# Column-group products in a different order: conditioning steps, state space outputs and the last gate

## Chip, core, metric

One Trainium2 chip, one core. The metric is the device time of one execution of the whole block in microseconds (us); the time before is the median of three runs, 1891.27 us.

## What is computed

A transformer-like block over 256 tokens and 2048 features, all in fp32. Cut to what the change touches:

```python
cond = silu(c) @ w_ada + b_ada                       # 2048 -> 6 x 2048
sh1, sc1, g1, sh2, sc2, g2 = split(cond, 6)
h = rmsnorm(x, norm1_g) * (1 + sc1) + sh1
u, q, kv, gates = split(h @ w_in, ...)
# state space mixer: (sr, si) is a complex scan along the 256 tokens
y = einsum('ghp,blgp->blgh', c_re, sr) - einsum('ghp,blgp->blgh', c_im, si) + d_skip * u
z = gelu(y); y_ssm = z * sigmoid(z @ w_glu + b_glu)
y_att = nsa_attention(q, kv, gates)                  # compressed, selected and window branches
x = x + g1 * (concat(rmsnorm(y_ssm), rmsnorm(y_att)) @ w_out)
h2 = rmsnorm(x, norm2_g) * (1 + sc2) + sh2
x = x + g2 * peer(h2)                                # 16384 experts, top 16 of each of 8 heads
out = rmsnorm(x, final_g)
```

## The kernel before

The large products are made exact to fp32 by splitting each operand into two fp32r parts, hi and lo, and adding three products (hi hi, hi lo, lo hi). A weight unit of 128x1024 is loaded by the SP queue into a ring of four `raw` buffers, ScalarE casts hi (L99), VectorE subtracts for lo (L102), TensorE multiplies (L521, L582, L775, L1013).

Three kinds of products have few output rows and are plain fp32, which the hardware runs as two passes each:

- **Conditioning, `cond_job` (L441 to L458).** `silu(c)` is one vector, so each product has one useful output row. Column k of it stands in `scz` as a 128x32 stationary with zeros behind it, and the product of group g goes to PSUM partitions 32g to 32g+31 (`cps`). So four products, which belong to four slices of the contraction, use four different 32-column groups of the array; L475 or L468 adds the four rows later. A job (j, q) gives 512 of the 12288 outputs; it has four steps of four products, and each step reads two loaded units of 512 KB: `tiles[0:2]` come from unit p2, `tiles[2:4]` from unit p2+1 (`load_steps`, L418). 20 jobs make 80 steps. The units of the first jobs lie in several borrowed buffers (`adap`, `er`, `vN`, `hi`, `lo`, `adax`), those of the last twelve jobs in the three buffers `adap` alone. The first eight jobs are needed early, for `h`; the twelve others are fed in between other work by `pump`.
- **State space outputs, `s5_py` (L699).** One step handles four of 64 state groups. VectorE makes four rotated products p, q, a2, c2 in this order (L683 to L686, tiles `s1`, `s3`, `s4`, `s5`), GpSimd and VectorE share what comes before. Each of the four then gives a pair of 128*32 products into two column groups of `py` (L710): 16 steps of four pairs.
- **The last gate, `g2_job` (L1313).** The vector is the stationary itself (128x1), and four products go to PSUM partitions 0, 32, 64 and 96 (`psg`, L1318). Products 0 and 1 read the first unit `rs[0]`, products 2 and 3 the second unit `rs[1]`, both in the `raw` ring. There are 16 such steps, put between the tiles of the expert scores (`u_tile`, products `pa` of L521, with the gate groups `g_group`, `pgs` L1290).

What sets the order of work is the build itself: the program is recorded in the order in which Python runs it, and a scheduler with a simulated timeline then orders each engine's instructions by when their operands are ready on that timeline. TensorE, VectorE, ScalarE, GpSimd and the SP load queue each execute their own list strictly in that order. So a line that is written in another order moves rows on all engines.

Of the kernel before, what the change touches and what calls it, by code (L numbers as in the profile page):

```python
# [60 lines left out]
def build(tc, A):  # L61
    nc = tc.nc

    def bc(ap, shape):
        return ap.to_broadcast(list(shape))
# [20 lines left out]
    def unit(src, pool=None, tag="raw", bufs=4):  # L86
        if pool:
            r = pool.tile([128, 1024], F32, name=tag, tag=tag, bufs=bufs)
        else:
            r = buf("raw")  # L90
        i = nc.sync.dma_start(r, src)
        if tag.startswith("ada"):
            last["ada"] = i.ins
        return r
# [323 lines left out]
    def load_steps(n):  # L418
        while len(loaded) < min(n, len(loads)):
            s = len(loaded)  # L420
            j, q, p2 = loads[s]
            r = min(s // 8, len(rings) - 1)
            tiles = []
            for p in (p2, p2 + 1):
                b = rings[r][turns[r] % len(rings[r])]
                turns[r] += 1
                src = A["w_ada"][j, q, p]
                if isinstance(b, tuple):
                    x = unit(src, *b)
                    tiles += [x[:, :512], x[:, 512:]]  # L430
                else:
                    xs = spare(b)
                    for i, x in enumerate(xs):
                        w = 1024 // len(xs)
                        last["ada"] = nc.sync.dma_start(x, src[:, i * w:(i + 1) * w]).ins
                    tiles += xs if len(xs) == 2 else [xs[0][:, :512], xs[0][:, 512:]]
            loaded.append(tiles)
# [3 lines left out]
    def cond_job(j, q, late=0, ahead=0):  # L441
        ps = psM.tile([128, 512], F32, name="cps", tag="cps", bufs=1)
        for kt in range(0, KT, 4):
            load_steps(min(ran[0] + 1 + ahead, 32) if ahead else ran[0] + 1)
            tiles = loaded[ran[0]]
            assert loads[ran[0]] == (j, q, kt // 2)
            ran[0] += 1
            for g in range(4):
                nc.tensor.matmul(ps[32 * g:32 * g + 32, :], scz[:, kt + g], tiles[g],  # L449
                                 start=kt == 0, stop=kt == KT - 4)  # L450
            if kt == KT - 4:
                rows = base1.tile([128, 512], F32, name="rows", tag="rows", bufs=1)
                nc.scalar.copy(rows, ps)
            yield
        if late:
            finish.append([late, j, q, rows])
        else:
            cond_end(j, q, rows)  # L458
# [3 lines left out]
    def cond_end(j, q, rows):  # L462
        if j == 2:
            b = base1.tile([1, 1024], F32, name="row", tag="adap", bufs=3)[:, :512]
            cs = slice(q * 512, (q + 1) * 512)
            nc.gpsimd.dma_start(b, A["b_row"][0:1, cs])
            ps = psM.tile([1, 512], F32, name="psr", tag="mm", bufs=1)
            nc.tensor.matmul(ps, sel4, rows, start=True, stop=True)  # L468
            nc.vector.tensor_tensor(out=b, in0=b, in1=ps, op=OP.add)
            nc.gpsimd.dma_start(g1d[:, cs], b)  # L470
        else:
            i = {0: 0, 1: 1, 3: 2, 4: 3}[j]
            ps = psM.tile([128, 4], F32, name="pscol", tag="mm", bufs=1)
            for b in range(4):
                nc.tensor.matmul(ps[:, b:b + 1], rows[:, b * 128:(b + 1) * 128], sel4, start=b == 0, stop=b == 3)  # L475
            ks = slice(4 * q, 4 * q + 4)
            o = cond[:, i, ks]
            nc.vector.tensor_tensor(out=o, in0=ps, in1=bada[:, j, ks], op=OP.add)
            if j in (1, 4):
                nc.vector.scalar_tensor_tensor(o, o, 1.0, ng[:, j // 4, ks], op0=OP.add, op1=OP.mult)  # L480
# [11 lines left out]
    for j in (1, 0):  # L492
        for _ in cond_job(j, 0, ahead=4):
            pass
    h_quarter(0)

    def jobs(todo):
        for j, q in todo:
            yield from cond_job(j, q, late=2)
# [92 lines left out]
    def parts():  # L592
        for q in range(1, 4):
            for j in (1, 0):
                yield from cond_job(j, q, ahead=3)
            h_quarter(q)
# [18 lines left out]
    quad = {}  # L615

    def tl(tag):
        return s5t.tile(SHP, F32, name=tag, tag=tag, bufs=1)

    def rot(j0):  # L620
        return [bc(E[:, j0:j0 + 2].unsqueeze(2), SHP) for E in (Er, Ei)]
# [35 lines left out]
    def s5_out(n):  # L657

        jq, half = divmod(n, 2)
        j0 = 2 * n  # L660
        a, c = quad.pop(n)
        w = s5t.tile([128, 2, 2, 2], F32, name="zi0", tag="zi0", bufs=2)

        def scans(h):
            for ri, src in enumerate((a, c)):
                for i in range(2):
                    init = 0.0 if h == 0 else w[:, 1, ri, i:i + 1]
                    v.tensor_tensor_scan(out=src[:, i, h], data0=bc(mag[:, j0 + i:j0 + i + 1], [128, 128]),
                                         data1=src[:, i, h], initial=init, op0=OP.mult, op1=OP.add)
        scans(0)  # L670
        zr1, zi1 = a[:, :, 0, 127], c[:, :, 0, 127]
        c1, s1 = E128[:, 0, j0:j0 + 2], E128[:, 1, j0:j0 + 2]
        t = s5t.tile([128, 2, 2], F32, name="zt", tag="zt", bufs=2)
        v.tensor_tensor(out=w[:, 0, 0], in0=zr1, in1=c1, op=OP.mult)
        v.tensor_tensor(out=w[:, 0, 1], in0=zi1, in1=s1, op=OP.mult)
        v.tensor_tensor(out=t[:, 0], in0=zr1, in1=s1, op=OP.mult)
        v.tensor_tensor(out=t[:, 1], in0=zi1, in1=c1, op=OP.mult)
        v.tensor_tensor(out=w[:, 1, 0], in0=w[:, 0, 0], in1=w[:, 0, 1], op=OP.subtract)
        v.tensor_tensor(out=w[:, 1, 1], in0=t[:, 0], in1=t[:, 1], op=OP.add)
        scans(1)  # L680
        er, ei = rot(j0)
        p, q, a2, c2 = tl("s1"), tl("s3"), tl("s4"), tl("s5")
        v.tensor_tensor(out=p, in0=a, in1=er, op=OP.mult)  # L683
        v.tensor_tensor(out=q, in0=c, in1=ei, op=OP.mult)
        v.tensor_tensor(out=a2, in0=a, in1=ei, op=OP.mult)
        v.tensor_tensor(out=c2, in0=c, in1=er, op=OP.mult)  # L686
        quad["pq", n] = (0, p), (2, q), (1, a2), (1, c2)

    zs = {"todo": [], "go": False}

# [105 lines left out]
    def s5_step(k):  # L796

        if k < 16 and k % 2 == 0:
            quad["CP", k // 2] = s5_c(k // 2)
        late = k < 16 and k not in POOL_PAIRS and k and k - 1 not in POOL_PAIRS  # L800
        if k < 16 and k not in POOL_PAIRS and not late:
            s5_in(k)
        if k + 1 in POOL_PAIRS:
            s5_in(k + 1)
        if k:
            s5_out(k - 1)
            done.append(k - 1)
        while done:
            s5_py(done.pop())
        if late:  # L810
            s5_in(k)
# [280 lines left out]
    for k in range(0, KT, 2):  # L1092
# [7 lines left out]
        for i in range(2):  # L1100
            p = ps[:, i].rearrange("p a t -> p (a t)")
# [211 lines left out]
    def g2_job():  # L1313
        for kt in range(KT):
            rs = [unit(A["w_g2"][kt * 128:(kt + 1) * 128, h * 1024:(h + 1) * 1024])
                  for h in range(2)]
            for g in range(4):
                nc.tensor.matmul(g2ps[32 * g:32 * g + 1, :], scol[:, kt:kt + 1],  # L1318
                                 rs[g // 2][:, g % 2 * 512:(g % 2 + 1) * 512], start=kt == 0, stop=kt == KT - 1)
            yield  # L1320

    def g2_end(pool):
        rows = pool.tile([128, 512], F32, name="g2r", tag="g2r")
        for g in range(4):
# [3 lines left out]
            nc.gpsimd.dma_start(g2d[:, cs], rows[r])  # L1328

    g2 = g2_job()  # L1330
    while state["t"] < T:
        for _ in range(2):
# [408 lines left out]
```

## Time and profile before

| what | value |
|---|---|
| three runs | 1888.39, 1891.27, 1891.78 us, median 1891.27 |
| the profiled execution, its own time | 1887.95 us |
| its span, first to last instruction | 1886.1 us |
| TensorE (PE) busy | 1781.8 us, 94% |
| VectorE (DVE) busy | 1381.6 us, 73% |
| ScalarE (ACT), GpSimd (POOL) busy | 804.6 and 824.4 us |
| mean granted TensorE clock | 0.978 of 2.4 GHz |
| moved by DMA | 436.8 MB, 232 GB/s on average |

A row of the timeline gives start and duration; matmuls overlap, so what one costs TensorE is the distance from its start to the start of the next one. In time the kernel goes: 0 to 50 us first conditioning jobs and the transposes of x; 50 to 160 first half of the input projection with six more jobs; 160 to 400 the rest of it with the state space steps and the compression; 400 to 600 attention, output projection and the last conditioning jobs; 600 to 880 the expert queries and the first expert score tiles; 880 to 1312 score tiles with gate groups and the g2 steps; then the last score tiles, and from 1420 us on the gathered expert values.

### The profile page before, as it was taken

The numbers are of one execution on the slowest core, as the hardware profiler recorded it, in microseconds if no ns is written. First come the engines' busy times: TensorE is split into PE (matmuls) and PEld (weight loads), VectorE is DVE, ScalarE is ACT, GpSimd is POOL, SyncE is SP. The second block draws the span as 40 slices with busy tenths as digits, with TensorE's granted clock in tenths as the row PEclk, the third lists the DMA queues.
The fourth block names the chain that finished last, engine by engine and source line by source line (L and its number), as shares of the span: only waits on it lengthen the run. The fifth ranks groups of instructions, "written<-read, shape, count | busy, mean of one in ns | idle before, by whom it ended". The sixth has DMA issues, their size and how long they took to land. (4 is left out here: it accounts for less than half of the span.)

```text
span 1886.1 us, 32604 instructions
## 1 busy us (share of the span) xinstructions
PE 1781.8 (94%) x12048; PEld 1488.0 (79%) x12048; DVE 1381.6 (73%) x2765; ACT 804.6 (43%) x1329; POOL 824.4 (44%) x926
## 2 busy tenths in 40 slices
PE   5999999999999899999999999999998999999895
PEld 2756655568666899999999898898998898777674
DVE  3636998756745698888999898998783457776666
ACT  3422211148634544444444444444432336555554
POOL 5923432201110210112787666665027665887532
PEclk9998999999999999999999999999998999999998
DMA  9987556785686455555565556556567779999972
GB/s 358 407 286 265 192 185 226 260 314 199 238 268 208 166 180 179 171 178 167 184 194 193 190 183 196 184 178 201 182 186 218 227 233 356 323 326 323 373 258 109
DMA packets 117839, 436.77 MB, mean 232 GB/s; under 512 B 17237, under 2 KB 19989, under 8 KB 107686
## 3 DMA queue, kind: packets, MB, share of 16 engines
q1 hardware_dynamic: 91440, 322.41, 51.3%
q0 software_dynamic: 22080, 108.62, 16.2%
q10 hardware_dynamic: 4150, 3.56, 0.6%
q8 instruction: 97, 1.59, 0.3%
q14 instruction: 72, 0.59, 0.1%
HBM read 411.38 MB, written 23.15 MB: 230 GB/s over the span
## 5 line engine op out<-in xcount | busy, mean ns | idle before, releaser
L102 DVE TENSOR_TENSOR lo<-raw,hi 128x1024 fp32r<-128x1024 f32 x382 | 512.9, 1345 | 229.6 <-ACT hi L99 188.3
L99 ACT CAST hi<-raw 128x1024 fp32r<-128x1024 f32 x385 | 402.1, 1047 | 590.7 <-PE pa L521 302.2
L521 PE MATMUL pa<-hhi,lo 128*128 128x256 f32 x2048 | 590.3, 288 | 10.1 <-DVE lo L102 6.7
L521 PE MATMUL pa<-hhi,hi 128*128 128x256 f32 x2048 | 583.6, 285 | 9.7 <-ACT hi L99 6.8
L521 PE MATMUL pa<-hlo,hi 128*128 128x256 f32 x2048 | 583.1, 285 | 0.0
L521 PEld LDWEIGHTS pa<-hhi,lo 128*128 128x128 f32 x2048 | 395.0, 193 | 38.3 <-DVE lo L102 11.1
L521 PEld LDWEIGHTS pa<-hhi,hi 128*128 128x128 f32 x2048 | 395.3, 193 | 10.8 <-ACT hi L99 8.0
L521 PEld LDWEIGHTS pa<-hlo,hi 128*128 128x128 f32 x2048 | 395.3, 193 | 0.5 <-issue 0.5
L1287 POOL TENSOR_TENSOR mv<-o,gp 128x256 fp32r<-128x256 f32 x256 | 186.4, 748 | 124.9 <-DVE o L1284 65.8
L1505 DVE TENSOR_TENSOR lv<-rv,hv 128x1024 fp32r<-128x1024 f32 x144 | 173.1, 1229 | 55.7 <-ACT hv L1504 52.3
L1504 ACT CAST hv<-rv 128x1024 fp32r<-128x1024 f32 x144 | 146.3, 1049 | 63.6 <-DMA rv<-in_peer_v,wt 40.7
L1284 DVE TENSOR_TENSOR o<-pT,iota 128x256 fp32r<-128x256 f32 (+1 forms) x256 | 124.8, 502 | 30.8 <-PE pgs L1290 17.9
L449 PE MATMUL cps<-adap,scz 128*32 128x512 f32 x476 | 113.8, 622 | 16.4 <-DMA adap<-in_w_ada 16.4
L1205 POOL TENSOR_TENSOR eq<-eq,iff 128x512 f32<-128x512 f32 x16 | 30.0, 1896 | 212.1 <-DVE eq L1204 212.1
L1305 POOL TENSOR_TENSOR SA<-SA,gs 128x50 f32<-128x50 f32 (+42 forms) x128 | 113.8, 904 | 12.9 <-ACT SA L1162 12.5
L1414 POOL DMA_INDIRECT wc<-SA,slot x88 | 97.1, 1103 | 46.1 <-issue 25.2
L1459 POOL DMA_INDIRECT rv<-in_peer_v,wt x74 | 97.3, 1316 | 45.2 <-DVE lv L1505 17.5
L521 PE MATMUL lin<-hhi,hi 128*128 128x256 f32 x352 | 104.8, 298 | 2.2 <-ACT sg L998 1.3
L521 PE MATMUL lin<-hlo,hi 128*128 128x256 f32 x352 | 102.9, 292 | 1.5 <-POOL hlo L1111 1.0
L521 PE MATMUL lin<-hhi,lo 128*128 128x256 f32 x352 | 102.6, 292 | 0.0
L1295 ACT COPY gs<-pgs 128x256 f32<-128x256 f32 x128 | 47.6, 373 | 121.7 <-POOL SA L1305 107.5
L521 PEld LDWEIGHTS lin<-hhi,hi 128*128 128x128 f32 x352 | 68.1, 194 | 26.3 <-issue 16.9
(450 smaller groups left out, 3291.9 us busy)
## 6 DMA issues: line engine op xcount, KB each, us to landing
raw<-in_peer_u SPq DMA_DIRECT2D x256, 512.0 KB
adap<-in_w_ada SPq DMA_DIRECT2D x119, 512.0 KB
raw<-in_w_in SPq DMA_DIRECT2D x32, 512.0 KB
raw<-in_w_out SPq DMA_DIRECT2D x32, 512.0 KB
raw<-in_peer_wq SPq DMA_DIRECT2D x32, 512.0 KB
raw<-in_w_g SPq DMA_DIRECT2D x32, 512.0 KB
raw<-in_w_inq SPq DMA_DIRECT2D x16, 512.0 KB
raw<-in_cmp_w SPq DMA_DIRECT2D x16, 512.0 KB
```

Source lines behind the costliest of these rows:

```text
L99: i = nc.scalar.copy(hi[:, :n], raw[:, :n])
L102: (lo_engine or nc.vector).tensor_tensor(out=lo[:, :n], in0=raw[:, :n], in1=hi[:, :n].bitcast(F32), op=OP.subtract)
L449: nc.tensor.matmul(ps[32 * g:32 * g + 32, :], scz[:, kt + g], tiles[g], start=kt == 0, stop=kt == KT - 4)
L521: nc.tensor.matmul(ps, w, a[:, kk], start=first and u == 0 and k == 0 and i == 0, stop=last and u == n - 1 and k == 7 and i == 2)
L1284: nc.vector.tensor_tensor(out=o, in0=bc(pT[:, j, t:t + 2].unsqueeze(2), shp), in1=io, op=OP.is_equal)
L1287: nc.gpsimd.tensor_tensor(out=mv[:, :, j], in0=o2, in1=g, op=OP.mult)
L1295: nc.scalar.copy(tmp, pv[:, 1])
L1305: nc.gpsimd.tensor_tensor(out=o, in0=o, in1=tmp[:, a0:m], op=OP.mult)
L1414: d = nc.gpsimd.indirect_dma_start(out=wcs[i], out_offset=bass.IndirectOffsetOnAxis(ap=ap, axis=0), in_=SB[:, m - NSA] if i else SA[:, m], ...
L1459: d = nc.gpsimd.indirect_dma_start(out=raw, out_offset=None, in_=A["peer_v"], in_offset=bass.IndirectOffsetOnAxis(ap=wt[:, 128:129].bitcas ...
L1504: nc.scalar.copy(hi, raw)
L1505: state["last"] = nc.vector.tensor_tensor(out=lo, in0=raw, in1=hi.bitcast(F32), op=OP.subtract).ins
```

## The change

Three loops are written in another order. In the conditioning step and in the g2 step the two products of the second unit come first, then those of the first: groups 2, 3, 0, 1. In the state space step the pair of c2, which VectorE makes last, comes first: c2, p, q, a2. Which products there are and what each reads and writes is the same; only `start` and `stop` follow the same step numbers as before, and the sum of the four state space pairs is taken in another order.

```diff
@@ cond_job @@
-            for g in range(4):
+
+            for g in (2, 3, 0, 1):
                 nc.tensor.matmul(ps[32 * g:32 * g + 32, :], scz[:, kt + g], tiles[g],
                                  start=kt == 0, stop=kt == KT - 4)
@@ s5_out @@
-        quad["pq", n] = (0, p), (2, q), (1, a2), (1, c2)
+        quad["pq", n] = (1, c2), (0, p), (2, q), (1, a2)
@@ g2_job @@
-            for g in range(4):
+            for g in (2, 3, 0, 1):
                 nc.tensor.matmul(g2ps[32 * g:32 * g + 1, :], scol[:, kt:kt + 1],
                                  rs[g // 2][:, g % 2 * 512:(g % 2 + 1) * 512], start=kt == 0, stop=kt == KT - 1)
```

The lines after the first edit move down by one (L449 becomes L450, L710 L711, L1318 L1319).

TensorE in the g2 stage, the first of 16 steps (the others moved in the same way). `psg` are the g2 products (raw_9167 is the first unit, raw_9169 the second), `pa` the score products. Before, the first pair:

```order
L521 MATMUL pa_8983<-hhi_90,hi_8979 128x256
L521 MATMUL pa_8983<-hlo_91,hi_8979 128x256
L1318 MATMUL psg_8840<-raw_9167,scol_77 1x512 x2
L521 MATMUL pa_8983<-hhi_90,lo_8980 128x256
L521 MATMUL pa_8983<-hhi_90,hi_8979 128x256
```

and, 26 rows after it, the second:

```order
L1290 MATMUL pgs_8848<-mv_8843,o1_8841 128x256 x2
L521 MATMUL pa_8983<-hhi_90,lo_8980 128x256
L521 MATMUL pa_9081<-hhi_90,hi_9071 128x256
L521 MATMUL pa_9081<-hlo_91,hi_9071 128x256
L1318 MATMUL psg_8840<-raw_9169,scol_77 1x512 x2
L521 MATMUL pa_9081<-hhi_90,lo_9072 128x256
```

Now:

```order
L522 MATMUL pa_9081<-hhi_90,hi_9071 128x256
L522 MATMUL pa_9081<-hlo_91,hi_9071 128x256
L1291 MATMUL pgs_8848<-mv_8843,o1_8841 128x256 x2
L1319 MATMUL psg_8840<-raw_9169,scol_77 1x512 x2
L1319 MATMUL psg_8840<-raw_9167,scol_77 1x512 x2
L522 MATMUL pa_9081<-hhi_90,lo_9072 128x256
L522 MATMUL pa_9081<-hhi_90,hi_9071 128x256
```

All four products stand next to each other, near the place where the second pair stood.

TensorE in the attention stage, steps of conditioning job cps_4084, before (`lin` is the output projection, `ppt`, `plg`, `psq` are attention and norm products):

```order
L978 MATMUL psq_4511<-ones_92,sqt_4080 128x1
L449 MATMUL cps_4084<-adap_4184,scz_411 32x512 x2
L978 MATMUL psq_4511<-ones_92,sqt_4080 128x1
L982 MATMUL psq_4511<-ones_92,sq_4558 128x1 x2
L1013 MATMUL lin_4572<-hi_4795,mhi_4001 128x512
L449 MATMUL cps_4084<-adap_4236,scz_411 32x512 x2
L923 MATMUL ppt_4581<-ident_70,lg_4461 128x128 x4
L895 MATMUL plg_4734<-kvT_104,uq_103 128x256 x2
L449 MATMUL cps_4084<-adap_4238,scz_411 32x512 x2
```

and now:

```order
L924 MATMUL ppt_4577<-ident_70,lg_4447 128x128 x2
L979 MATMUL psq_4511<-ones_92,sqt_4080 128x1 x2
L983 MATMUL psq_4511<-ones_92,sq_4558 128x1 x2
L450 MATMUL cps_4084<-adap_4184,scz_411 32x512 x2
L450 MATMUL cps_4084<-adap_4182,scz_411 32x512 x2
L924 MATMUL ppt_4581<-ident_70,lg_4461 128x128 x4
L896 MATMUL plg_4734<-kvT_104,uq_103 128x256 x2
```

The pairs of a step, which stood apart, now stand together; the next step (adap_4238, adap_4236) follows as one block too.

TensorE in the state space stage, one step, before (`s1`, `s3`, `s4`, `s5` hold p, q, a2, c2; `lin` is the input projection):

```order
L521 MATMUL lin_2382<-hhi_90,hi_2166 128x256
L710 MATMUL py_2230<-s1_2222,CP_2021 32x256 x2
L521 MATMUL lin_2382<-hlo_91,hi_2166 128x256
L521 MATMUL lin_2382<-hhi_90,lo_2167 128x256
L521 MATMUL lin_2382<-hhi_90,hi_2166 128x256
L710 MATMUL py_2230<-s3_2223,CP_2021 32x256 x2
L710 MATMUL py_2230<-s4_2224,CP_2021 32x256 x2
L710 MATMUL py_2230<-s5_2225,CP_2021 32x256 x2
```

and now:

```order
L522 MATMUL lin_2382<-hhi_90,lo_2167 128x256
L711 MATMUL py_2230<-s5_2225,CP_2021 32x256 x2
L711 MATMUL py_2230<-s1_2222,CP_2021 32x256 x2
L711 MATMUL py_2230<-s3_2223,CP_2021 32x256 x2
L711 MATMUL py_2230<-s4_2224,CP_2021 32x256 x2
L522 MATMUL lin_2382<-hhi_90,hi_2166 128x256
```

Eleven of the 16 steps have their four pairs in a row now, one had before. In two of the other five the pairs have 10 and 16 rows of other work between them: VectorE's list moved too and makes c2 first there.

Call a stretch a run of such narrow products (`cps`, `py`, `psg`, and the compression's `ph` of L743) with no wider product between. TensorE's list has 161 of them before and 110 now: 31 and 24 in the early jobs (50 to 160 us), 58 and 42 in the state space and compression stage, 33 and 22 in the attention stage, 32 and 16 in the g2 stage. SP's list of loads changes up to the output projection's weights and is the same after it; there the two `adap` loads of a step now stand next to each other nearly everywhere.

## Rows read from the trace of the kernel before

**Rows 1.** The page: TensorE's share of the span, and of the slices of 47 us each TensorE and DMA (tenths).

```profile
PE 1781.8 (94%) x12048; PEld 1488.0 (79%) x12048; DVE 1381.6 (73%) x2765; ACT 804.6 (43%) x1329; POOL 824.4 (44%) x926
...
PE   5999999999999899999999999999998999999895
...
DMA  9987556785686455555565556556567779999972
```

**Rows 2.** Busy time by stage: from, to, length; busy us and count of PE, PEld (weight loads), DVE, ACT, POOL; then granted TensorE clock (1.00 is 2.4 GHz), mean DMA share, GB/s.

```profile
50.00:160.00 110.00, 104.79 (x667) 68.01 (x668) 51.09 (x61) 31.79 (x41) 54.75 (x46) 0.95 0.90 333
160.00:400.00 240.00, 231.50 (x1536) 146.18 (x1534) 202.87 (x431) 55.33 (x81) 76.95 (x75) 0.98 0.65 227
400.00:600.00 200.00, 197.75 (x1062) 142.08 (x1062) 113.28 (x247) 111.65 (x232) 19.51 (x21) 1.00 0.72 246
...
880.00:1312.00 432.00, 426.29 (x3350) 390.49 (x3349) 391.57 (x855) 193.20 (x411) 295.02 (x383) 1.00 0.59 189
```

**Rows 3.** Timeline of TensorE around one pair of the g2 stage: start us, duration us. An x4 is two products of two passes.

```profile
915.57 0.28 PE L521 MATMUL pa<-hhi,hi 128*128 128x256 f32 x1
915.69 0.28 PE L521 MATMUL pa<-hlo,hi 128*128 128x256 f32 x1
915.90 1.03 PE L1318 MATMUL psg<-raw,scol 128*1 128x512 f32 x4
916.85 0.39 PE L521 MATMUL pa<-hhi,lo 128*128 128x256 f32 x1
917.08 0.28 PE L521 MATMUL pa<-hhi,hi 128*128 128x256 f32 x1
```

**Rows 4.** Timeline of TensorE around one conditioning step whose four products (x8) happened to stand together.

```profile
214.66 0.28 PE L521 MATMUL lin<-hhi,lo 128*128 128x256 f32 x1
214.87 1.06 PE L449 MATMUL cps<-adap,scz 128*32 128x512 f32 x8
215.86 0.38 PE L521 MATMUL lin<-hhi,hi 128*128 128x256 f32 x1
216.09 0.28 PE L521 MATMUL lin<-hlo,hi 128*128 128x256 f32 x1
```

**Rows 5.** Timeline of TensorE where several steps of four products follow one another.

```profile
45.18 0.62 PE L449 MATMUL cps<-er,scz 128*32 128x512 f32 x2
45.19 0.62 PE L449 MATMUL cps<-vN,scz 128*32 128x512 f32 x2
45.63 0.60 PE L449 MATMUL cps<-er,scz 128*32 128x512 f32 x2
...
46.06 0.60 PE L449 MATMUL cps<-adap,scz 128*32 128x512 f32 x2
```

**Rows 6.** Timeline of TensorE at a single state space pair (x4), and at a step whose four pairs stood together (x16).

```profile
203.06 0.63 PE L710 MATMUL py<-s,CP 128*32 128x256 f32 x4
203.62 0.39 PE L521 MATMUL lin<-hhi,lo 128*128 128x256 f32 x1
...
321.25 1.92 PE L710 MATMUL py<-s,CP 128*32 128x256 f32 x16
323.10 0.69 PE L631 MATMUL pq<-uq,Ball 32*128 32x256 f32 x2
```

**Rows 7.** The costliest groups, that of the g2 products: busy us, mean ns of one pass, idle before and what ended it.

```profile
L1318 PE MATMUL psg<-raw,scol 128*1 128x512 f32 x128 | 32.8, 591 | 4.6 <-DMA raw<-in_w_g 4.2
```

**Rows 8.** What TensorE waited for (us in total, times, longest): the first row of the answer for 50 to 160 us, the first two for 160 to 400, the first for 400 to 600, and all (two) for 880 to 1312.

```profile
PE cps L449 <- DMA adap<-in_w_ada: 2.2, 1, 2.2
...
PE cps L449 <- DMA adap<-in_w_ada: 2.6, 3, 1.4
PE py L710 <- DVE s L684: 1.6, 1, 1.6
...
PE lin L521 <- ACT sg L998: 1.3, 1, 1.3
...
PE psg L1318 <- DMA raw<-in_w_g: 4.2, 6, 1.2
PE pa L521 <- DVE lo L102: 0.7, 3, 0.3
```

**Rows 9.** What the SP load queue waited for, in the same form: two rows for 50 to 160 us, one for 160 to 400, one for 400 to 600, one for 880 to 1312.

```profile
SPq L91 <- PE cps L449: 34.2, 18, 6.6
SPq L435 <- PE cps L449: 13.9, 11, 2.4
...
SPq L91 <- PE cps L449: 58.4, 22, 10.0
...
SPq L91 <- PE cps L449: 64.7, 27, 4.7
...
SPq L91 <- PE psg L1318: 53.6, 32, 2.9
```

**Rows 10.** What VectorE waited for, 880 to 1312 us: the two largest rows.

```profile
DVE o L1284 <- PE pgs L1290: 17.9, 26, 1.9
DVE o L1284 <- POOL mv L1287: 10.6, 15, 1.4
```

**Rows 11.** Timeline of the load queue and of TensorE at one g2 step: the issue of its two loads (the second 2.2 us after the first) and the first pair, which waited for the first load.

```profile
1074.25 2.55 SPq L91 DMA_DIRECT2D raw<-in_w_g  x2
...
1078.17 1.03 PE L1318 MATMUL psg<-raw,scol 128*1 128x512 f32 x4 [0.52 <-DMA raw<-in_w_g]
```

## The prediction

> **What bounds the kernel now.** I read the shares and slices of the page first, then the stages, then TensorE's timeline at the products in question, then who waits for whom. TensorE is busy for 94% of the span, and its slices are full from about 50 us on except near the end [rows 1]. By stage it leaves idle 5 us of 110, 8 of 240, 2 of 200 and 6 of 432 [rows 2], and the waits found there are single ones, the largest 4.2 us in all [rows 8]. So from 50 to 1312 us TensorE takes its list nearly without a stop, and time taken out of that list comes back as time of the kernel as long as nothing else is late. The first 50 us are different: DMA is 90% busy and TensorE half idle [rows 1]; I count nothing for the change there.
>
> **What a narrow product costs.** In the g2 stage a wide product follows the last at 0.12 us (915.57 to 915.69). The pair starts 0.21 after its predecessor, the next wide product comes 0.95 after that, and the one behind it 0.23 later [rows 3]. Against steps of 0.12 that is 0.95 + 0.09 + 0.11 = 1.15 us for two products. A conditioning step whose four products stood together takes 0.21, 0.99 and 0.23 in the same places, so 1.19 us for four products [rows 4]: the four column groups run at once, and the second pair is almost free. Where steps follow one another each takes 0.88 us (45.18 to 46.06), two passes of 0.44 [rows 5]; so I price a stretch of narrow products as its length on the array, 0.87 us for each full slot, plus 0.32 us for entering and leaving (1.19 less 0.87). A state space pair alone takes 0.56 us and four pairs in a row 1.85 [rows 6]: 0.43 for each pair, since consecutive pairs use the same two groups, and the rest once per stretch. There only the 0.32 us per stretch is to be had, unless a conditioning pair shares the other groups.
>
> The Trainium skill would price the joining lower. "TensorE: Matmul & The Clock Gate", section "Measured speedup vs the span model", reports 2.38 times for three column groups, 0.79 of the ideal. Were each quad slowed in that proportion, it would last about 1.25 us instead of 0.99 (an estimate from that page), some 40 joined steps would return 0.26 us less each, and the forecast would be 10 us later. This case's row shows 0.99 us for four groups against 0.95 for two, so the measurement decides.
>
> **The change, part by part.** The number of products stays; the places change.
> - *g2 steps, 880 to 1312 us.* 32 stretches become 16, each step two pairs at 1.15 turned into one quad at 1.19: 2.30 - 1.19 = 1.11 us, times 16 = **17.8 us**. The 128 passes in [rows 7] confirm that all pairs are of that one kind. The waits: now the first product of a step needs the second load, issued 2.2 us after the first [rows 11]. The quad stands 23 rows later than the first pair did, 23 x 0.12 = 2.8 us, so it finds its load about as ready as before, and the 4.2 us of DMA wait [rows 8] should stay near that size. The first unit's buffer is freed some 3 us later; SP already waits 53.6 us there for these products [rows 9], and the score tiles behind wait on TensorE for nothing but 0.7 us of VectorE [rows 8], so that is covered. What may eat gain is VectorE, busy 391.6 of 432 us [rows 2]: 40 us idle, of which 28.5 are waits for TensorE's gate products and GpSimd's multiply [rows 10]. With 18 us less there are 22 left. Bounds: 22 (the 4.2 us of wait goes too) and 8 (VectorE's chain of gate groups sets the pace for half of it). I take 15, nearer to the full sum because TensorE waits only 0.7 us for VectorE now [rows 8].
> - *Conditioning in attention, 400 to 600 us.* 33 stretches with 35 slots become 22 with 22: 13 x 0.87 + 11 x 0.32 = **14.8 us**. Here the products are also filler between attention's dependent steps, whose VectorE and ScalarE parts are not shorter; where lists are shorter, a softmax may end late instead. The three `adap` buffers matter too: a quad frees two at once, so of the next quad only one unit can be there early. SP waits 64.7 us for these products to free buffers, with other loads behind it in its list [rows 9]. Bounds 0 and 14.8; VectorE at 57% and TensorE with no wait above 1.3 us [rows 2, 8] put it near the upper end: I take 11.
> - *State space and compression, 160 to 400 us.* 58 stretches become 42, and the length on the array falls from 83.7 to 75.9 us: 7.8 + 16 x 0.32 = **12.9 us**. VectorE is busy 202.9 of 240 us [rows 2], and the scans are one long chain on it. The outputs now start when c2 is there and take 1.85 us from then instead of 0.56; the next user of p's buffer comes only after the next eight scans, so that is hidden, but `u` becomes ready some 1.3 us later in every second step. Bounds 0 (VectorE's chain sets the stage) and 12.9: I take 8.
> - *Early jobs, 50 to 160 us.* 31 stretches become 24, 38 slots 33: 5 x 0.87 + 7 x 0.32 = **6.6 us**. DMA is at 0.90 [rows 2], yet SP waits 34.2 + 13.9 us for conditioning products to free its buffers [rows 9], so the stage is bound by both in turn: half, 3.
> - Casts, subtractions, scans, other loads: the same instructions. The lists of all engines are rearranged up to 600 us; I price that at 0 with a spread of several us either way, which the range holds.
>
> Sum: 15 + 11 + 8 + 3 = 37 of a possible 52.1. The profiled execution took 1887.95 us, so 1851; the median of the runs lies 3.3 us above it, and I say **1853**.
>
> **Rivals.**
> 1. *Only the g2 stage pays.* Before 600 us DMA, the scans and the softmax chain take the room that TensorE gives up. For it: VectorE 85% busy in the state space stage, DMA 0.90 before it. Against: the almost waitless TensorE there. Then 1887.95 - 16 = 1872.
> 2. *All of it comes back.* 1887.95 - 52.1 = 1836. For it: [rows 8]. Against: that no other engine becomes late in 52 us less.
> 3. *Slower: loads exposed at the head of the list.* The first product of a step is now the one whose unit lands last, and everything behind it on TensorE waits. From issue to use a load takes 3.9 us (1074.25 to 1078.17) [rows 11]; with three buffers the second unit of a step is issued only when the step before has run. The place is the 48 steps of the last twelve jobs, 160 to 600 us, 9 us apart on average but in bursts. If each waits 1.1 us the gain of 52.1 is gone; at 1.5 us it is 72 - 52 = 20 us slower, 1908. Against: these waits are 2.6 us in all now [rows 8], and 9 us is more than twice 3.9. The Trainium skill says in the same page, section "The mechanism", that matmuls are strictly first in, first out; that is what gives this rival its force, and [rows 11], where a pair waits for its load, agrees.
> 4. *It does not do what it says, or the rearranged lists cost what the joining gives.* Five state space steps are still apart, and every engine's list has moved before 600 us. About 1888, within several us.
>
> **How the numbers follow.** Forecast, 1840 to 1866: 0.52. Rival 1, 1866 to 1880: 0.22. Rival 2, below 1840: 0.13. Rival 3: 0.08. Rival 4: 0.05, of which 0.02 on the faster side. The range for 8 in 10 goes from the full sum, 1835, to a g2 stage that pays 10 us, 1878; outside lie rivals 3 and 4 and the lower half of rival 2. Faster by over 0.2% (3.8 us, about what a measurement of this kernel tells from no change): 0.52 + 0.22 + 0.13 + 0.02 = 0.89; within it 0.03; slower 0.08.
>
> **What would show it.** Right: `psg` as 16 rows of x8 at 0.99 us; TensorE's busy time down by some 45 us; the g2 stage some 15 us shorter, with VectorE nearer to full; the stretch from 50 to 600 us some 22 us shorter; everything from 1312 us on shifted but not changed. Wrong: quads of 1.8 us; new waits of `cps` for `adap` of over 1 us each; or the place of the last state space output unmoved while TensorE idles before it.

## The result, and the profile after

| kernel | median us | lowest to highest | runs |
|---|---|---|---|
| before | 1889.83 | 1880.28 to 1891.78 | 4 |
| changed | 1865.43 | 1862.85 to 1870.28 | 4 |

The ratio is 0.9891, 95% interval 0.986 to 0.9922: faster by 24 us. Forecast were 1853 and a range of 1835 to 1878, so the sign and the range held, and of the 37 us forecast about two thirds came. The median lies 0.6 us inside the bracket that the forecast claimed for itself (1840 to 1866). The profiled execution took 1870.28 us, the slowest of its four.

The page of the changed kernel, busy time in us and share of the span; against [rows 1] TensorE has 40.0 us less, and VectorE 21 more:

```profile
PE 1741.8 (93%) x12048; PEld 1487.8 (80%) x12048; DVE 1402.7 (75%) x2765; ACT 800.0 (43%) x1325; POOL 825.5 (44%) x926
```

The windows by stage, columns as in [rows 2] (busy of PE, PEld, DVE, ACT, POOL, then clock, DMA share, GB/s). The last window is moved to where the g2 stage is now:

```profile
50.00:160.00 110.00, 98.80 (x660) 69.59 (x656) 54.74 (x58) 31.30 (x41) 52.71 (x44) 0.94 0.85 310
160.00:400.00 240.00, 226.83 (x1579) 150.05 (x1572) 215.73 (x440) 58.77 (x86) 71.63 (x76) 0.97 0.68 240
400.00:600.00 200.00, 192.93 (x1086) 146.13 (x1086) 117.81 (x248) 107.38 (x231) 18.25 (x22) 0.99 0.75 252
869.00:1288.00 419.00, 412.41 (x3351) 389.93 (x3350) 398.82 (x855) 194.83 (x411) 297.63 (x383) 1.00 0.60 194
```

TensorE idles now 11 us of 110, 13 of 240, 7 of 200 and 7 of 419, against 5, 8, 2 and 6 in [rows 2]. VectorE is at 90% in the state space stage (85% before) and at 95% in the g2 stage (91%).

TensorE's timeline at a g2 step (start us, duration us), to be read beside [rows 3] and [rows 4]:

```profile
982.99 0.40 PE L1291 MATMUL pgs<-mv,o 128*128 128x256 f32 x2
983.32 1.04 PE L1319 MATMUL psg<-raw,scol 128*1 128x512 f32 x8
984.29 0.39 PE L522 MATMUL pa<-hhi,lo 128*128 128x256 f32 x1
984.51 0.28 PE L522 MATMUL pa<-hhi,hi 128*128 128x256 f32 x1
```

Four products in 0.97 us (983.32 to 984.29), where two took 0.95. All 16 steps stand like this.

What TensorE waited for (us in all, times, longest), first rows of the answers for 50 to 160, 160 to 400, 400 to 600 and 869 to 1288 us:

```profile
PE pscol L476 <- ACT rows L454: 4.1, 5, 1.9
PE lin L583 <- ACT kvT L586: 2.4, 1, 2.4
...
PE py L711 <- DVE s L687: 10.1, 3, 5.3
PE pq L632 <- DVE uq L570: 1.6, 1, 1.6
...
PE lin L522 <- ACT sg L999: 2.3, 1, 2.3
PE cps L450 <- DMA adap<-in_w_ada: 1.5, 2, 1.2
PE po L930 <- ACT PT L925: 1.2, 1, 1.2
PE lin L1014 <- ACT sg L999: 0.9, 1, 0.9
...
PE pa L522 <- DVE lo L102: 2.3, 8, 0.5
PE pgs L1291 <- POOL mv L1288: 2.0, 4, 0.5
PE psg L1319 <- DMA raw<-in_w_g: 1.4, 4, 0.7
```

Against [rows 8]: the g2 steps wait less for their loads than before (1.4 for 4.2 us), and 4.3 us of waits for VectorE and GpSimd stand in their place (0.7 before). In the state space stage `py` products wait 10.1 us for VectorE's last product c2 (L687), where they waited 2.9 us for p and q before.

VectorE in the g2 stage, what it waited for; the two waits of [rows 10], 28.5 us, are 12.9 now:

```profile
DVE o L1285 <- POOL mv L1288: 10.3, 20, 1.1
...
DVE o L1285 <- PE pgs L1291: 2.6, 5, 0.7
```

To see where the 24 us came from, I cut TensorE's timeline at four places: the last product of the projection quarters (`lin`, L582), of the glu product (L775), of the output projection (L1013), and of the last gate (`psg`). "Narrow" is the time that TensorE spent from the start of a `cps`, `py`, `ph` or `psg` product to that of the next instruction, less what it waited; "idle" is the gaps, without the time before TensorE's first product (11.6 us before, 13.1 now). All are sums over the rows of the timeline.

| stretch | before: us, narrow, idle | changed: us, narrow, idle | difference | forecast |
|---|---|---|---|---|
| to the last quarter | 124.9, 39.0, 12.7 | 136.5, 40.2, 18.4 | +11.6 | -3 |
| to the end of glu | 295.9, 115.4, 12.2 | 279.1, 96.8, 18.5 | -16.8 | -8 |
| to the end of the output projection | 179.4, 30.2, 2.2 | 173.2, 18.9, 7.1 | -6.2 | -11 |
| to the last gate's end | 707.9, 29.6, 13.8 | 695.2, 15.5, 13.0 | -12.7 | -15 |
| to the end | 560.8, 1.0, 34.5 | 567.2, 1.0, 39.2 | +6.4 | 0 |

Up to the last gate it is 24.2 us. The 6.4 us at the end are this one execution's: a second profile of the same kernel, below, takes 543.7 us there, and run 10, a version of the kernel before timed in the same group, 547.0.

How far one list repeats, run 1 below tells, which has every engine's list of the kernel before up to some 880 us. Its first three cuts come at 124.4, 417.3 and 596.8 us, those of the kernel before at 124.9, 420.8 and 600.2. So a difference of 3 us up to 600 us is within what two executions of one list differ by.

### The profile page after: what moved, and what is told of

It reads as the page before. It is cut to its first block, busy times and chain, and to the rows that moved or that the text cites. A ratio compares the mean times of both kernels' runs of the same rounds, so it can differ in the third digit from the quotient of the medians.

```text
span 1868.4 us, 32585 instructions
## 1 busy us (share of the span) xinstructions
PE 1741.8 (93%) x12048; PEld 1487.8 (80%) x12048; DVE 1402.7 (75%) x2765; ACT 800.0 (43%) x1325; POOL 825.5 (44%) x926
## 5 line engine op out<-in xcount | busy, mean ns | idle before, releaser
L522 PE MATMUL pa<-hhi,lo 128*128 128x256 f32 x2048 | 590.2, 288 | 14.7 <-DVE lo L102 10.1
L522 PEld LDWEIGHTS pa<-hhi,hi 128*128 128x128 f32 x2048 | 394.4, 193 | 11.5 <-ACT hi L99 6.0
L1288 POOL TENSOR_TENSOR mv<-o,gp 128x256 fp32r<-128x256 f32 x256 | 180.9, 727 | 111.3 <-DVE o L1285 71.9
L1505 ACT CAST hv<-rv 128x1024 fp32r<-128x1024 f32 x144 | 146.4, 1049 | 78.5 <-DMA rv<-in_peer_v,wt 59.2
L1285 DVE TENSOR_TENSOR o<-pT,iota 128x256 f32<-128x256 f32 (+1 forms) x256 | 132.3, 543 | 13.5 <-POOL mv L1288 10.3
L1306 POOL TENSOR_TENSOR SA<-SA,gs 128x50 f32<-128x50 f32 (+42 forms) x128 | 122.0, 968 | 10.8 <-ACT SA L1163 10.8
L1460 POOL DMA_INDIRECT rv<-in_peer_v,wt x74 | 102.6, 1387 | 41.7 <-issue 16.0
L450 PE MATMUL cps<-adap,scz 128*32 128x512 f32 x476 | 88.0, 625 | 1.9 <-DMA adap<-in_w_ada 1.9
```

Of the source, the lines that this page charges most:

```text
L522: nc.tensor.matmul(ps, w, a[:, kk], start=first and u == 0 and k == 0 and i == 0, stop=last and u == n - 1 and k == 7 and i == 2)
L1285: nc.vector.tensor_tensor(out=o, in0=bc(pT[:, j, t:t + 2].unsqueeze(2), shp), in1=io, op=OP.is_equal)
L1288: nc.gpsimd.tensor_tensor(out=mv[:, :, j], in0=o2, in1=g, op=OP.mult)
L1306: nc.gpsimd.tensor_tensor(out=o, in0=o, in1=tmp[:, a0:m], op=OP.mult)
L1460: d = nc.gpsimd.indirect_dma_start(out=raw, out_offset=None, in_=A["peer_v"], in_offset=bass.IndirectOffsetOnAxis(ap=wt[:, 128:129].bitcas ...
L1505: nc.scalar.copy(hi, raw)
```

## The experiments

Each was timed in four or five rounds beside the kernel before. The first four ran together, with 1889.27 us for the kernel before; in the later groups it took 1872.97, 1870.88 and 1871.07, so only ratios compare across groups.

**1 to 4: the parts alone.** The last gate's loop only:

```diff
@@ g2_job @@
-            for g in range(4):
+            for g in (2, 3, 0, 1):
```

> Only the g2 steps have the new order; conditioning and state space steps as before. Theory (array time of joined products comes back where TensorE's list is dense): about 13 to 15 us faster than before, all of it between the first and the last psg product, nothing before 880 us and nothing after 1312 us. Rival (VectorE, 91% busy there, sets the pace once TensorE's list is shorter): 8 us or less, with new TensorE waits for VectorE's lo.

1874.03 us, ratio 0.9925 (0.9902 to 0.9949). From the first product of the gate groups (`ppk`, L1258) to the last gate TensorE took 414.7 us, 427.5 before and 414.5 in the whole change: the g2 edit works by itself and is worth 13 us. In the profiles of all the runs below and the two kernels this stretch takes 414.1 to 414.7 us in the six with this edit and 427.5 to 430.4 in the eight without it.

The state space order only:

```diff
@@ s5_out @@
-        quad["pq", n] = (0, p), (2, q), (1, a2), (1, c2)
+        quad["pq", n] = (1, c2), (0, p), (2, q), (1, a2)
```

> Only the state space steps have the new order. Theory: only the price of a stretch is to be had there, at most 16 stretches x 0.32 us; 2 to 5 us faster, between 160 and 400 us. Rival (outputs wait for c2, so u is late and the scans or the gated unit behind it are): 0 to 5 us slower, with TensorE waits of py for VectorE as in the whole change (10 us there).

1891.29 us, ratio 1.0011 (0.999 to 1.0033). Its glu product ends at 416.2, 4.6 us before that of the kernel before and 1.1 before that of run 1, and its output projection at 600.2, as before: nothing is left. Its attention stretch holds 33.1 us of narrow products where the kernel before has 30.2.

The conditioning loop, once only for the steps after the first 32 and once only for the first 32:

```diff
@@ cond_job @@
-            for g in range(4):
+            for g in (2, 3, 0, 1) if ran[0] > 32 else (0, 1, 2, 3):    # late; early: ran[0] <= 32
```

> Only the last twelve conditioning jobs (160 to 600 us) have the new order; the first eight as before. Theory: 13 slots of 0.87 us and the stretches in attention, and some of the same among the state space steps: 12 to 18 us faster, no loss before 160 us. Rival (the softmax chain and three load buffers take it back): under 6 us faster.

1875.78 us, ratio 0.9937 (0.9916 to 0.9957). The output projection ends at 587.9 us, 12.3 us early (8.9 against run 1), which is as early as in the whole change.

> Only the first eight conditioning jobs (0 to 160 us) have the new order. Theory (a joined step holds TensorE's list and, through its buffers, SP's load list until both of its units are in, so projection units behind come late): 6 to 12 us slower than before, the last quarter product of L582 some 10 us later. Rival (the 11.6 us that the whole change lost there come from the other edits, by the rearranged lists): within 3 us of before.

1898.17 us, ratio 1.0044 (1.0021 to 1.0067): slower. The projection quarters end at 135.5 (124.9 before), the output projection at 609.1 (600.2). So the part forecast at 3 us of gain costs 8 to 9 by itself. Of the 10.6 us by which the quarters end late, 3.1 are there at their start (52.5 us instead of 49.4); the rest arises in them. The load queue tells what happens in the first stretch. Its issues in this kernel (start us, duration us), 67 to 87 us:

```profile
69.08 0.33 SPq L91 DMA_DIRECT2D er<-in_w_ada  x1
69.89 0.33 SPq L435 DMA_DIRECT2D adax<-in_w_ada  x1
70.33 0.37 SPq L91 DMA_DIRECT2D adap<-in_w_ada  x1
70.75 0.42 SPq L435 DMA_DIRECT2D adax<-in_w_ada  x1
71.26 0.38 SPq L91 DMA_DIRECT2D er<-in_w_ada  x1
71.70 0.42 SPq L91 DMA_DIRECT2D adap<-in_w_ada  x1
72.21 1.75 SPq L435 DMA_DIRECT2D adax<-in_w_ada  x2
74.02 0.66 SPq L91 DMA_DIRECT2D adap<-in_w_ada  x1
75.53 10.26 SPq L130 DMA_DIRECT2D raw<-in_w_inq  x4
```

and in the kernel before:

```profile
67.67 0.33 SPq L91 DMA_DIRECT2D er<-in_w_ada  x1
68.81 0.33 SPq L91 DMA_DIRECT2D adap<-in_w_ada  x1
70.08 0.33 SPq L130 DMA_DIRECT2D raw<-in_w_inq  x1
71.35 0.33 SPq L435 DMA_DIRECT2D adax<-in_w_ada  x1
72.58 0.33 SPq L130 DMA_DIRECT2D raw<-in_w_inq  x1
74.06 0.33 SPq L435 DMA_DIRECT2D adax<-in_w_ada  x1
74.49 0.37 SPq L91 DMA_DIRECT2D adap<-in_w_ada  x1
75.15 1.61 SPq L130 DMA_DIRECT2D raw<-in_w_inq  x2
```

Before, the projection's loads (`raw<-in_w_inq`) stand between the loads of a job. Now a whole job's loads stand first and the four projection loads behind them; the ninth projection load is issued at 75.53 instead of 62.69, the thirteenth at 95.28 instead of 76.43. Ahead of them SP waits once for TensorE for a long time (us in all, times, longest, 55 to 90 us, the kernel with the early edit; the same answer of the kernel before has 9.0, 4, 3.7):

```profile
SPq L91 <- PE cps L449: 8.1, 2, 7.7
```

TensorE runs the joined products there as one block, from 68.01 to 71.63 us on its timeline, and until it does their buffers are not free. The largest row of the same answer is another one: the projection's loads themselves wait 8.6 us for VectorE's `lo`, which has to be done with a `raw` buffer (2.8 in the kernel before). All but 0.8 us of that comes behind the block and adds to the lateness of the later units.

**5 and 6: without the early part.** The whole change with the late conditioning condition above, and the same without the state space edit.

> The change without its early part: the g2 edit, the state space edit, and the conditioning edit only after the first 32 steps. Theory (the early part alone costs some 9 us, the others add up): the g2 edit 14 to 15 us, the late conditioning steps 12 to 13, the state space edit 0: 1889 - 27 = about 1862, 3 to 8 us below the whole change; the last input projection quarter ends where it does in the kernel before. Rival (what is lost early is lost whatever comes first, because the stage from 160 to 400 us waits for VectorE and sets the end): 1869 to 1874, no better than the whole change.

1848.63 us, ratio 0.9868 (0.9848 to 0.9887).

> As the run before, and the state space steps in their old order too: only the g2 edit and the conditioning edit after the first 32 steps. Theory (the state space edit gives nothing that lasts): within 3 us of that run, about 1862. Rival (the state space edit and the joined conditioning steps help each other, since a conditioning pair beside a state space pair uses the other column groups): 4 us or more slower than that run.

1846.83 us, ratio 0.9853 (0.9836 to 0.987): the lowest ratio of all, though its interval overlaps that of run 5. The state space edit gives nothing here either, and no help between it and the joined steps shows.

**7 and 8: the projection's loads on another queue.** The early edit alone and, as a control, the kernel before, both with

```diff
@@ Units.load @@
-                    nc.sync.dma_start(r[:, :cols], src)
+                    (nc.scalar if 4 <= len(self.raw) < 16 else nc.sync).dma_start(r[:, :cols], src)
```

> The conditioning edit for the first 32 steps alone, which took 8 to 9 us more than the kernel before, and twelve loads of the input projection's first quarters (the fifth to the sixteenth use of the raw ring) issued by ScalarE's queue in place of SP's. Theory (those loads stand behind a whole job's conditioning loads in SP's list, and the projection's products wait for them): the loss is at most 3 us against the next run, which has the same queues without the edit. Rival (the joined steps hold TensorE itself, or its lower clock there): the loss against the next run stays at 8 to 10 us.

> The kernel before with the same twelve loads on ScalarE's queue: the control for the run before. Theory: SP's list lets these loads through early enough in the kernel before, so within 4 us of it, 1886 to 1893. Rival (SP's list holds them up there as well): faster by 5 us or more.

1884.71 us, ratio 1.0059 (1.0039 to 1.0079), and 1869.1, ratio 0.998 (0.9962 to 0.9999). The loss grew to 15 us, which neither theory expected. The test is confounded: the loads now stand in ScalarE's list, and where one waits there for a `raw` buffer, ScalarE's copies behind it wait too. TensorE's largest wait in this kernel, 40 to 145 us, is for such a copy:

```profile
PE lin L582 <- ACT kvT L585: 6.4, 1, 6.4
```

It decides nothing about SP's list.

**9 and 10: the loads mixed again.** The early edit alone and the kernel before, both with the loads of steps 13 to 32 ordered behind the projection load recorded before them (`inq` collects those loads):

```diff
@@ load_steps @@
-            for p in (p2, p2 + 1):
+            with tc.issue_after(inq[-1]) if 12 <= s < 32 else ExitStack():
+                for p in (p2, p2 + 1):
```

> The conditioning edit for the first 32 steps alone, as in the run that took 8 to 9 us more than the kernel before, but the loads of steps 13 to 32 stand in SP's list behind the weight load of the projection that was recorded before them. So the projection's loads stand between the loads of a job's steps again, and not behind all ten of them. Theory (the loss comes from SP's list: the projection's units are issued late, and TensorE then runs blocks of 12 and 13 conditioning products that waited for each other): no loss against the next run, which has the same rule of loads without the edit: from 4 us faster to 3 us slower, and the last projection quarter ends within 4 us of that run's. Rival (joined steps cost TensorE time here whatever SP's order is, because the first product of a step waits for the unit that lands last): still 8 us or more slower than the next run.

> The kernel before with the same rule for the loads of steps 13 to 32: the control for the run before. Theory: its list of loads is mixed already, so within 4 us of the kernel before. Rival (the rule itself moves the time): over 5 us either way.

1887.6 us, ratio 1.0099 (1.0075 to 1.0122), and 1878.87, ratio 1.0045 (1.0027 to 1.0062): the rule by itself costs 8 us, where at most 4 were expected. Half of the theory held: with mixed loads the last quarter ends at 128.0, 7.5 us sooner than with the early edit alone and 2.9 us sooner than in the control (130.9). Some 2.4 to 3 us of that are an earlier start; from first to last product the quarters take 78.5 us here, 79.0 in the control and 83.0 with the early edit alone. The other half fell: the kernel is still 9 us slower than its control. Its output projection ends at 610.2, that of the control, which was later at 131 us, at 600.0. So SP's list explains the longer quarters. It does not explain the loss of this kernel, which arises between 131 and 420 us, where it takes 300.2 us and its control 289.3; the early edit had moved every list there too.

About half of that loss goes with TensorE's clock. The windows of TensorE (from, to, length, busy us and count, granted clock, DMA share, GB/s) in the kernel with mixed loads:

```profile
131.00:420.00 289.00, 275.27 (x1745) 0.96 0.68 239
187.40:197.60 10.20, 9.66 (x40) 0.50 0.40 145
```

and in its control:

```profile
131.00:420.00 289.00, 274.87 (x1800) 0.99 0.71 251
187.40:197.60 10.20, 9.33 (x76) 1.00 0.40 142
```

The clock falls behind a wait for VectorE. In the window at 0.50, which is 1.2 GHz, a wide product follows the last at 0.21 us, where it is 0.12 at 1.00 [rows 3]:

```profile
186.04 0.63 PE L713 MATMUL py<-s,CP 128*32 128x256 f32 x4 [2.80 <-DVE s L686]
...
194.10 0.41 PE L524 MATMUL lin<-hhi,hi 128*128 128x256 f32 x1
194.32 0.41 PE L524 MATMUL lin<-hlo,hi 128*128 128x256 f32 x1
```

Between 131 and 420 us TensorE works 20 us at the lower clock in this kernel and 6.5 in its control. By the two distances the 13.4 us more cost 6 of the 11 (an estimate). Why the control has so little of it is not shown: the kernel before and the early edit alone both have 0.965 between 131 and 420 us, and the control 0.988.

**11: the changed kernel again**, unedited.

> The changed kernel again, in five rounds, for a narrower interval than the four runs of the result gave. If its parts add up as measured one by one (g2 edit 0.9925, state space edit 1.0011, late conditioning 0.9937, early conditioning 1.0044, product 0.9917): 0.991 to 0.993, over 0.4% above the same change without its early part (0.9853 and 0.9868). If the early loss is smaller beside the other parts than by itself: 0.987 to 0.989.

1846.21 us, ratio 0.9872 (0.9846 to 0.9899). The cuts come at 135.4, 417.3, 590.1 and 1284.9 us, within 1.7 us of the first profile; from there to the end it takes 543.7, and the two kernels without the early part 543.9 and 547.0. The product of the four ratios measured alone is 0.9917. The whole is lower, but the four intervals together leave some 0.0045 to either side of that product, so the times alone do not show that the parts fail to add up. The traces say more: the early part, which costs 9 us alone, costs 1 to 3 beside the others by the end of the output projection (588.8 and 590.1 with it, 587.9 and 586.9 without). By the time of the whole it can't be told: the intervals with it and without it overlap.

**12: does TensorE still set the time?** The whole change with less work in it:

```diff
@@ cond_job @@
+                n = 64 if ran[0] > 32 and kt else 512
-                nc.tensor.matmul(ps[32 * g:32 * g + 32, :], scz[:, kt + g], tiles[g],
+                nc.tensor.matmul(ps[32 * g:32 * g + 32, :n], scz[:, kt + g], tiles[g][:, :n],
```

> The whole change, and in the twelve late conditioning jobs the three later steps of four multiply only the first 64 of their 512 columns (the other 448 outputs of these steps' slices are left out). Loads, waits and order rules stay; TensorE gets up to 36 steps x some 0.8 us = 29 us less to do before the end of the output projection. Theory (with the steps joined, TensorE no longer sets the time from 125 to 600 us: what it is spared there turns into waits for VectorE, ScalarE and the lists): the end of the output projection comes at most 10 us earlier than in the changed kernel (589 us), and the time is 0.982 to 0.988 of the kernel before. Rival (TensorE still sets it, and the joined steps gave less than forecast because they cost more than the 1.19 us of the one row): 20 us or more come back, 0.978 or less.

2268.04 us; that time is not to be read: with the left-out conditioning the experts differ, and its page has 180 gathers of expert values (`rv`) in one group where the page of the kernel before has 74. Up to the output projection the late jobs are not used yet, and there the theories differ. TensorE's timeline, the last row of the output projection, in the kernel before:

```profile
600.24 0.63 PE L1013 MATMUL lin<-hi,mlo 128*128 128x512 f32 x2
```

in the changed kernel:

```profile
588.75 0.63 PE L1014 MATMUL lin<-hi,mlo 128*128 128x512 f32 x2
```

and in this one:

```profile
562.24 0.63 PE L1015 MATMUL lin<-hi,mlo 128*128 128x512 f32 x2
```

26.5 us earlier than in the changed kernel. The theory (at most 10) fell and the rival (20 or more) held in its time; its reason, that a joined step costs more than the 1.19 us of the one row, is not what was found (next section). What was taken out is shown by the windows of `cps` alone (the first figure behind the length is TensorE's busy time), 0 to 620 us, in the kernel before:

```profile
0.00:620.00 620.00, 140.24 (x640) 21.70 (x640) 11.69 (x20) 0.98 0.74 263
```

in the changed kernel:

```profile
0.00:620.00 620.00, 109.57 (x640) 18.72 (x640) 11.64 (x20) 0.96 0.74 263
```

and in this one:

```profile
0.00:620.00 620.00, 75.34 (x640) 18.29 (x640) 11.70 (x20) 0.96 0.75 271
```

From the changed kernel to this one 34.2 us of TensorE's work went and 26.5 us of time, 77%; TensorE's idle time up to there stayed, 44.0 and 44.5 us. From before to the changed kernel 30.7 us went and 11.5 us of time: 37% (8.0 us and 27% against run 1); the idle time rose from 27.2 to 44.0.

The same three rows show the granted clock: 0.98 before, 0.96 in the other two. Up to the output projection TensorE works 27 us at the lower clock in the kernel before, and 39 and 42 in the two profiles of the changed kernel. By the distances of 0.12 and 0.21 that costs 5 to 7 us (an estimate), which no term of the forecast held. It is 28 to 46 us in the nine profiles with an edit of the conditioning steps and 18 to 30 in the five without. One place is common to the nine: between 182 and 191 us a `py` product has waited 2.8 to 6.2 us for VectorE, and in that wait or just behind it the clock falls to 0.50 for a few us. In the five others no such wait stands there, and the clock is at 1.00 from 160 to 240 us. So in this kernel such a wait cost its own length and the slower work behind it.

## Why the prediction held, and where it was wrong

**The bound: right in the main.** TensorE's list sets the time up to 600 us, also after the change; the last experiment shows it, with 77% of what was taken out, where I had come to doubt it.

**The price of a joined step: right on the array.** 0.97 us for four products against the 0.99 of [rows 4]. So the slower quads that the Trainium skill's 2.38 times would have given ("TensorE: Matmul & The Clock Gate", "Measured speedup vs the span model"; estimate 1.25 us) did not occur. That the forecast by that estimate, 10 us later than mine, lies nearer to the result is chance: the missing time is not in the quads.

**g2: the mechanism right, 15 sized as 13.** From the first `ppk` (L1258) to the last gate three profiles give 13.0, 13.4 and 12.8 us (427.5 before; 414.5, 414.1 and 414.7). The narrow products gave 15.1 (30.6 to 15.5 by the timeline) of the 17.8 summed; the shorter waits for loads, which I had expected to stay, gave 2.8 more (4.2 to 1.4); the new waits for VectorE and GpSimd took 3.6 (0.7 to 4.3), and the score products between them 1.4 (357.1 to 358.5). So what the forecast counted for entering and leaving a stretch, some 3 us of the 17.8, did not come back, and that 13 came so near to 15 owes something to the 2.8 us of load waits, which the prediction had in its upper bound alone. VectorE being the next to be late was named, and it is.

**Attention: 11 forecast, 6 came.** 11.3 of the 14.8 us came off the narrow products, and TensorE's idle time rose by 4.9. By the rows of waits from 400 to 600 us it is 3.2 us for `sg`, the sigmoid of the glu (1.3 before), 1.5 for `adap` loads (none before) and 1.2 for the copy behind the softmax. The bounds of that term named the softmax and the three load buffers; the sigmoid, the largest of the three, they did not.

**State space and early jobs: 8 and 3 forecast; together 5.2 came**, 3.5 in the second profile, and against run 1 1.9 and 0.2: little or nothing. Here a step failed: "The lists of all engines are rearranged up to 600 us; I price that at 0", and with it the early jobs as half of 6.6. The joining freed most of what I counted (narrow time to the end of glu 154.4 to 137.0 us, 17.4 of the 19.5 summed). But with the new lists come waits: up to there TensorE idles 12.0 us more, of it 7.2 before `py` products for VectorE, 4.1 before `lin` and 3.5 before `pscol`, while it waits 3.4 less for conditioning loads. The last state space outputs hardly moved, before and now:

```profile
395.04 1.49 PE L710 MATMUL py<-s,CP 128*32 128x256 f32 x12
...
394.05 1.92 PE L711 MATMUL py<-s,CP 128*32 128x256 f32 x16
```

They end at 396.5 and 396.0 us (393.0 in run 1, 397.7 in the second profile): what the joining freed up to there made up for the 11.6 us by which the quarters end late, and no more. In run 6, where they end on time, it is 391.7. The longer `py` waits do not come from putting c2 first. Run 3, with the old order in the state space step, has 10.3 us of them from 160 to 400 us:

```profile
PE py L710 <- DVE s L683: 7.8, 4, 4.7
PE py L710 <- DVE s L684: 2.5, 2, 2.1
```

Run 2, with the new order alone, has 3.4; so they come with the conditioning edit, and with them the lower clock told above. Early on, the longer quarters fit SP's list, by the load rows and the mixed loads. The prediction took SP's list by its two sums of waits [rows 9] and did not ask whose loads come to stand behind whose.

**Rivals.** Rival 3 (loads exposed at the head of the list) did not come where I put it: the late steps wait 1.9 us in all for `adap`. The nearest to it is the early stage, with the queue in place of the load: not a product that waits for its unit, but other loads that wait behind. Rival 2 failed for the idle time, rival 1 because the late conditioning steps pay 9 to 12 us.

**Signs.** TensorE's busy time fell by 40 us (45 forecast), the g2 stage by 13 (15), the stretch up to 600 us by 11.5 (22). Of the signs of being wrong one came: the last state space outputs are where they were, and TensorE idles before `py` (though that stage began late). Waits of `cps` for `adap` reach 1.2 us once from 400 to 600 us, 1.5 in two, against the over 1 us each that was named. The last step of the sum, 1851 and 3.3, makes 1854 and not 1853.

**Open.** Why the early edit alone costs 9 us by 600 us. Its quarters end 10.6 us late, which is as much, and SP's list fits that. But with the loads mixed the quarters are not late, and the loss comes behind them, some 6 of 11 us with a lower clock. Beside the late edit the same late quarters (136.5 us, and 135.4 in the second profile) are in part or wholly made up for by the end of glu: 415.6 and 417.3, where the two kernels without the early part have 417.5 and 411.9. No run tells whether one cause stands behind the three.

## What to carry to other kernels

Joining products that use different column groups is worth its price per stretch where the rest of the list stays (13 of 17.8 us in the g2 stage). Where a scheduler rebuilds every list, read the new order before pricing the gain: in the load queue, whose loads now stand behind whose, and for which engine each joined block waits; here 8 to 11.5 of 30.7 us came back. Read the granted clock beside the idle time: here the work behind a long wait ran at half the clock. A part that costs 9 us alone cost 1 to 3 beside the others, so leave a part out of the whole as well as testing it alone. And take two profiles of one list before reading a difference of 3 us.

## What was not expected of the hardware

The clock of the first work differs between runs of the same list. From 40 to 50 us the granted clock was 0.83 before and 0.54 in the changed kernel, which looks like an effect of the joining; but the runs 5 and 10, whose early steps are not edited, show 0.50, and runs 3, 6 and 1, which have the same early steps, show 0.83, 0.80 and 0.91. TensorE had been busy for 4.9 to 6.6 of the 10 us before that, at 0.83 to 0.86, in all five. In runs 5 and 10 the projection quarters begin 2.5 to 3.0 us later (52.4 and 51.9 us instead of 49.4), and by 600 us that is gone (587.9 us in run 5 and in run 3).

What follows the last gate took 557.6 to 567.2 us in the result and the first four experiments, and 543.5 to 547.0 in the later groups, whichever kernel it was (the last experiment aside); the stretches before it repeat, for the changed kernel, to within 1.7 us. It is not the gathers: the last score tiles (`pa`) take 266 to 269 us from the last gate in the result and the first four and 241.4 in the later ones, and what comes behind them, with the gathered values, 291 to 298 and 302 to 306. Windows of TensorE behind the last gate, in the kernel before (result) and the changed kernel (run 11):

```profile
1308.60:1548.60 240.00, 224.38 (x1758) 0.96 0.68 209
...
1285.40:1525.40 240.00, 238.79 (x1972) 1.00 0.79 236
```

The cause is open. A comparison between groups would have read 16 us of that as an effect.
